# Two-layer streaming encoder, one core: every transfer on SP's queue in program order, stores issued four units late, bias lines made on GpSimd

## The chip, the core and the metric

The kernel runs on one core of a Trainium2 chip. The core has five engines with a queue of instructions each: TensorE (PE in the rows: matmuls, with the weight loads as PEld), VectorE (DVE), ScalarE (ACT), GpSimd (POOL) and SyncE (SP), which here issues the DMA transfers. An engine works through its queue in the order in which the program was built; an instruction that waits for another engine holds up what stands behind it. The metric is the device time of one execution in microseconds, and lower is better.

## The reference, cut to what matters

One inference step of a two-layer encoder, for 256 prompt frames and 32 sample frames together (288 tokens, 1024 features).

```python
# layer 0: 8 heads of chunked attention with a bias by clipped distance (A), 8 heads of stick-breaking (B)
rel  = clip(q_loc[:, None] - k_loc[None, :], -128, 128) + 128
bias = rel_bias[rel]                      # (head, query, key)
s    = q @ k.T * HEAD_DIM ** -0.5 + bias
p    = softmax(where(valid, s, NEG_INF));  out = p @ v
# layer 1: 16 heads of forgetting attention
log_f = log_sigmoid(z + b_f);  cum = cumsum(log_f)
s    = q @ k.T * HEAD_DIM ** -0.5 + cum[q] - cum[k]
# each layer then: 4-head cross-attention into 256 memory tokens, SwiGLU FFN; a final RMSNorm
```

Keys and values of both layers, the log-forget values, and the memory's keys and values are outputs too, beside the activations.

## The kernel before, in words

**Tiling.** Features lie on the 128 partitions and tokens along the free axis, in eight blocks `x[0..7]` of 128x288. A weight matrix is read in **units**: one 128x1024 float32 tile of 512 KB, the eight 128x128 blocks that make one block of 128 output features. `unit` (L132) loads a unit into a buffer `st` (four of them), ScalarE rounds it to `hi` (L141), and VectorE subtracts to get the rest, `lo` (L142). `project` (L151) multiplies it with the activations, which are split the same way: for each of 8 blocks three matmuls, hi times hi, hi times the activations' rest, and lo times hi, so 24 matmuls of 128x288 to a unit.

**What runs between units.** Attention is written as generators. After each unit `project` calls `tick` (L176), which takes one step of every active generator. A step of `attend_prompt` (L359) for a pair of heads: transposes of the values (`vt`) and scores (`sc`), with the softmax on VectorE and ScalarE; one tick later transposes of the weights (`tp`, copied out by ScalarE as `pt`); one tick later the product with the values (`po`). For every second pair, `attend_sample` does the same for the sample frames (`ss`, `ts`, `os`). In `pairs` (L807) eight pairs of heads follow each other: units q, k and v of a pair, then its attention is made active, then units of the memory's keys or values (`Memory.step`, L544).

**What sets the order.** The order in which each engine's instructions stand is not the order of the Python text. The framework schedules the built program by its own costs, engine by engine, and may move an instruction ahead of others where its operands are ready earlier. That holds for SP's transfers also: a load can be put ahead of a store that was written before it.

**The bias of layer 0.** `rel_lines` (L735) makes, for each of 8 heads, a line of 384 values, and writes it 128 times to DRAM, each time shifted by one (`skew`, 385 values to a row), so that a diagonal band can be read as a rectangle. It is called after the first unit of layer 0: SP loads the line (L739), VectorE fills its clipped part (L740), SP stores it (L742) and issues eight copies (L745). `rel_prompt` (L753) reads two rectangles to a head, 128x128 and 128x256, and GpSimd masks two corners.

**The gate of layer 1.** `gate` (L821) takes the forget-gate unit (w[24]) through transposes on PE (`gt`), absolute value, exponential and logarithm on ScalarE and a chain of small VectorE operations to `lf`; SP stores `lf` (L848, L849); after two ticks PE sums it up (`gc`, `gs`, `gn`), VectorE copies the sums out, SP stores them (`cumd`, `cumsd`, L858, L865), and every pair of heads loads its lines from there (`ck`, L896). GpSimd makes the bias tiles (`bc`, L901 to L904).

Of the kernel before, what the change touches and what calls it, by code (L numbers as in the profile page):

```python
# [22 lines left out]
FB = 22  # L23


@with_exitstack
def encoder_step(ctx: ExitStack, tc: tile.TileContext, a):
# [15 lines left out]
    cnt = [0]  # L43

# [31 lines left out]
    def first_part(c0, c1):  # L76
        DMA.dma_start(first[:, c0:c1], a["w_ab"][0][:, c0:c1])

    first_part(0, 256)
    for i in range(4):  # L80
        DMA.dma_start(xh[i], a["xT"][:, 2 * i * NT:2 * (i + 1) * NT])
        if i == 0:
            DMA.dma_start(gain, a["gains"])
            first_part(256, 512)
        if i == 1:
            first_part(512, 1024)
# [5 lines left out]
    make_identity(nc, identb)  # L92

# [23 lines left out]
    for h in range(4):  # L117
        G.memset(odd[32 * h:32 * h + 32, h % 2:h % 2 + 1], 1.0)

# [12 lines left out]
    def unit(src, st=None, pieces=1):  # L132

        if st is None:
            st = wp.tile([P, 1024], F32, tag="st", bufs=4, name=name("st"))
            DMA.dma_start(st, src)
# [48 lines left out]
    def finish():  # L185
        while active:
# [153 lines left out]
    def softmax(s, cols, bias, out):  # L340
# [3 lines left out]
        for i, (c0, c1) in enumerate(cols):  # L344
# [4 lines left out]
            else:  # L349
                V.tensor_tensor_reduce(out=out[:, c0:c1], in0=s[:, c0:c1], in1=bias[:, c0:c1], scale=-1.0, scalar=3e38,  # L350
# [8 lines left out]
    def attend_prompt(q, k, v, vns, j, bias, oh, ol):  # L359

        vn = vns[j] = v_natural(v)
        e = []
        for hd in range(2):
# [5 lines left out]
            softmax(s, QT, bias[hd], e[hd])  # L369
# [134 lines left out]
    def cache(src):  # L504
        t = wk.tile([P, 512], F32, tag="ca", bufs=4, name=name("ca"))
        DMA.dma_start(t, src)
# [12 lines left out]
    class Memory:  # L519
# [5 lines left out]
        def prepare(self):  # L525

            for c in range(2):
                st = wp.tile([P, 1024], F32, tag="st", bufs=4, name=name("mem"))
                DMA.dma_start(st, a["memT"][:, 1024 * c:1024 * c + 1024])
# [14 lines left out]
        def step(self):  # L544
            i, l = self.i, self.l
            self.i += 1
            if i < 8:
# [5 lines left out]
                DMA.dma_start(a["mkT"][l, i], t[:, 0:NP])  # L553
                self.k.append(split(t[:, 0:NP], tok("kh", F32R)[:, 0:NP], tok("kl", F32R)[:, 0:NP]))
            else:
# [13 lines left out]
                if half == 1:  # L569
                    for t in range(2):  # L570
                        v = tok("mv")
                        V.tensor_scalar(v[:, 0:NP], self.p[:, 256 * t:256 * t + 256], memcol[:, t:t + 1], None, op0=ALU.mult)
                        DMA.dma_start(a["mv"][l, t, :, hd * 256:hd * 256 + 256], v[:, 0:NP])
# [151 lines left out]
    def evac_kv(cur, p, dst):  # L725
        t = tok("kv")

        def go():
            V.tensor_tensor(t, p[:, :NT], cur.r, ALU.mult)
            DMA.dma_start(dst, t)  # L730
# [4 lines left out]
    def rel_lines():  # L735


        ln = cst.tile([8, 384], F32, name="line")
        DMA.dma_start(ln[:, 128:384], a["rel"][:, 0:256])  # L739
        V.tensor_copy(ln[:, 0:128], ln[:, 128:129].to_broadcast([8, 128]))  # L740
        d = dr.tile([8, 384], F32, name="lined")
        DMA.dma_start(d, ln)  # L742
        sk = dr.tile([8, 128 * 385], F32, name="skew")
        for h in range(8):
            DMA.dma_start(bass.AP(tensor=sk.tensor, offset=sk.offset + h * 128 * 385, ap=[[385, P], [1, 384]]),  # L745
                          bass.AP(tensor=d.tensor, offset=d.offset + 384 * h, ap=[[0, P], [1, 384]]))
        return sk

    def rel_rows(sk, h, c, rows, n):

# [306 lines left out]
```

## Time and profile before

| what | us |
|---|---|
| median of 3 runs (970.48 to 972.98) | 971.6 |
| the profiled execution, its own time | 974.15 |
| its span, first to last instruction | 972.3 |
| PE busy in the span | 955.3 |
| DVE busy | 588.6 |
| ACT busy | 484.8 |
| POOL busy | 195.1 |

The profile is of one execution. Busy time of PE counts matmuls from start to end, and these overlap, so a share near 100% says that PE had work, not that it ran at its best rate. TensorE's granted clock was 1 in all but the stretches that the prediction shows. Of the span, some 70 us at the front and some 40 us at the start of layer 1 hold nearly all of PE's idle time.

### The profile page before, as it was taken

To read this page: it belongs to the slowest core of one execution; us is meant where nothing else is said; L and a number is where in the kernel's file an instruction comes from. 1 tells how busy PE (TensorE), PEld (TensorE's weight loads), DVE (VectorE), ACT (ScalarE), POOL (GpSimd) and SP (SyncE) were. 2 spreads that over 40 slices of the span, in tenths; PEclk is the share of its full clock that TensorE was granted. 3 is DMA by queue.
4 is the path that set the end of the run, shared out by engine and by line. 5 is a ranking of instruction groups with operands and counts; after the bars stand their busy time and mean duration, and the time that the engine had idled before them with its cause. 6 is when DMAs were issued, how large, how long until landed. Compare 5 with 4: busy or idle time off the path is not lost.

```text
span 972.3 us, 19122 instructions
## 1 busy us (share of the span) xinstructions
PE 955.3 (98%) x7495; PEld 923.2 (95%) x7495; DVE 588.6 (61%) x1133; ACT 484.8 (50%) x856; POOL 195.1 (20%) x291
## 2 busy tenths in 40 slices
PE   8999999999999999999999999999999999999997
PEld 7889999998999999999998999999989999999996
DVE  6587555676666555754565666657757655555452
ACT  5456768545554444444444545446546544444331
POOL 3021001310213222411004333213002222222010
PEclk9999999999999999999999999999999999999999
DMA  7775455544254444554555555555434444444431
GB/s 232 247 241 189 137 180 181 183 162 147 103 174 154 173 162 164 191 192 160 173 202 161 179 190 191 169 164 179 150 117 159 159 159 173 163 164 173 165 117 49
DMA packets 59721, 163.59 MB, mean 168 GB/s; under 512 B 8192, under 2 KB 20528, under 8 KB 59632
## 3 DMA queue, kind: packets, MB, share of 16 engines
q1 hardware_dynamic: 59632, 162.38, 49.0%
q8 instruction: 59, 0.97, 0.4%
q14 instruction: 30, 0.25, 0.1%
HBM read 152.20 MB, written 11.72 MB: 169 GB/s over the span
## 4 chain that ended last, share of the span: by engine, by line
PE 91%; DMA 3%; DVE 3%; issue 1%; ACT 1%; SPq 1%; POOL 0%; DVEq 0%; POOLq 0%; ACTq 0%
PE pj L68 51%; PE dn L68 14%; PE op L68 11%; PE mv L68 5%; PE po L68 1%; PE xo L68 1%; PE xs L68 1%; DMA st<-w_ab 1%; PE zb L68 1%; PE sc L68 1%; DVE lo L142 1%; DMA skew<-lined 1%; DMA x<-xT 1%; PE xss L68 1%; PE xt L614 0%
## 5 line engine op out<-in xcount | busy, mean ns | idle before, releaser
L141 ACT CAST hi<-st 128x1024 fp32r<-128x1024 f32 x260 | 272.2, 1049 | 335.7 <-issue 147.3
L68 PE MATMUL pj<-hh,hi 128*128 128x288 f32 (+1 forms) x1352 | 406.3, 301 | 0.0
L68 PE MATMUL pj<-hl,hi 128*128 128x288 f32 (+1 forms) x1352 | 399.9, 296 | 1.7 <-DVE hl L250 1.7
L68 PE MATMUL pj<-hh,lo 128*128 128x288 f32 (+1 forms) x1352 | 400.2, 296 | 0.0
L142 DVE TENSOR_TENSOR lo<-st,hi 128x1024 fp32r<-128x1024 f32 x260 | 322.7, 1242 | 127.4 <-PE dn L68 41.2
L68 PEld LDWEIGHTS pj<-hh,hi 128*128 128x128 f32 x1352 | 257.0, 190 | 5.8 <-issue 4.2
L68 PEld LDWEIGHTS pj<-hl,hi 128*128 128x128 f32 x1352 | 257.1, 190 | 3.3 <-DVE hl L250 3.2
L68 PEld LDWEIGHTS pj<-hh,lo 128*128 128x128 f32 x1352 | 256.9, 190 | 0.0
L68 PE MATMUL dn<-fh,hi 128*128 128x288 f32 x400 | 108.5, 294 | 0.0
L68 PE MATMUL dn<-fh,lo 128*128 128x288 f32 x352 | 103.3, 294 | 0.0
L68 PE MATMUL dn<-fl,hi 128*128 128x288 f32 x304 | 89.5, 294 | 0.0
L68 PE MATMUL op<-ol,hi 128*128 128x288 f32 x256 | 75.8, 297 | 0.0
L68 PE MATMUL op<-oh,hi 128*128 128x288 f32 x256 | 75.5, 297 | 0.0
L68 PE MATMUL op<-oh,lo 128*128 128x288 f32 x256 | 75.2, 294 | 0.0
L68 PEld LDWEIGHTS dn<-fh,hi 128*128 128x128 f32 x400 | 72.3, 188 | 0.0
L68 PEld LDWEIGHTS dn<-fh,lo 128*128 128x128 f32 x352 | 66.2, 188 | 0.0
L213 POOL TENSOR_TENSOR ssq<-ssq,sq 128x288 f32<-128x288 f32 (+1 forms) x37 | 37.7, 1018 | 119.8 <-ACT sq L202 76.8
L68 PEld LDWEIGHTS dn<-fl,hi 128*128 128x128 f32 x304 | 57.1, 188 | 0.0
L695 POOL TENSOR_TENSOR fl<-us,fh 128x288 fp32r<-128x288 f32 x38 | 32.9, 865 | 119.3 <-ACT fh L694 119.3
L690 DVE TENSOR_TENSOR us<-pj,rstd 128x288 f32<-128x288 f32 x44 | 20.1, 457 | 59.9 <-PE pj L68 59.9
L691 POOL TENSOR_TENSOR gs<-gs,sg 128x288 f32<-128x288 f32 x44 | 38.9, 884 | 75.8 <-ACT sg L689 75.8
L68 PEld LDWEIGHTS op<-ol,hi 128*128 128x128 f32 x256 | 48.2, 188 | 0.6 <-issue 0.4
(257 smaller groups left out, 1204.9 us busy)
## 6 DMA issues: line engine op xcount, KB each, us to landing
st<-w_gate SPq DMA_DIRECT2D x44, 512.0 KB, 3.3
st<-w_up SPq DMA_DIRECT2D x44, 512.0 KB, 3.2
st<-w_down SPq DMA_DIRECT2D x44, 512.0 KB, 3.2
st<-w_c SPq DMA_DIRECT2D x25, 512.0 KB, 3.3
st<-w_ab SPq DMA_DIRECT2D x23, 512.0 KB, 4.4
st<-w_xk SPq DMA_DIRECT2D x16, 512.0 KB, 3.4
st<-w_xv SPq DMA_DIRECT2D x16, 512.0 KB, 3.5
st<-w_xq SPq DMA_DIRECT2D x16, 512.0 KB, 3.5
```

Source lines behind the costliest of these rows:

```text
L68: T.matmul(out, lhsT, rhs, start=start, stop=stop, skip_group_check=True)
L141: S.copy(hi[:, b], st[:, b])
L142: V.tensor_tensor(lo[:, b], st[:, b], hi[:, b].bitcast(F32), ALU.subtract)
L213: eng.tensor_tensor(s[:, :self.n], self.acc[i][:, :self.n], q[:, :self.n], ALU.add)
L690: V.tensor_tensor(us, pu[:, :NT], cur.r, ALU.mult)
L691: G.tensor_tensor(gs, gs, sg, ALU.mult)
L695: G.tensor_tensor(lo, us, hi.bitcast(F32), ALU.subtract)
```

## The change

Four things are done, and the program is scheduled anew.

1. Every transfer that SP issues goes through `move`, which keeps them in the order of the program text (`keep_in_program_order`).
2. The stores of keys, values and memory outputs are put off by four units: `store` puts them on a list of four, and each `tick` issues the oldest entry. `finish` ticks until the list is empty.
3. The bias lines of layer 0 are made at the very front, by GpSimd's own DMA queue and GpSimd's own copy. A head's line is written 64 times and not 128, in two copies of four heads each; a head reads two rectangles of 64x256, and both query tiles take their bias from one 128x256 tile (offsets 128 and 0).
4. Memory preparation is made active just ahead of the third pair's units and not behind the second pair's, the first pair of layer 1 starts one tick later (`later`), the bias tiles of layer 0 are loaded at the attention's first step, and `y` is stored in three transfers and not six.

```diff
+    def move(dst, src):
+        tc.keep_in_program_order(DMA.dma_start(dst, src))
...
+    G.dma_start(line[:, 128:384], a["rel"][:, 0:256])
...
+    G.tensor_copy(line[:, 0:128], line[:, 128:129].to_broadcast([8, 128]))
+    G.dma_start(lined, line)
+    for h in range(0, 8, 4):
+        G.dma_start(bass.AP(tensor=skew.tensor, offset=skew.offset + h * SKEW, ap=[[SKEW, 4], [385, 64], [1, 384]]),
+                    bass.AP(tensor=lined.tensor, offset=lined.offset + 384 * h, ap=[[384, 4], [0, 64], [1, 384]]))
...
             st = wp.tile([P, 1024], F32, tag="st", bufs=4, name=name("st"))
-            DMA.dma_start(st, src)
+            move(st, src)
...
+        for f in stores.pop(0):
+            f()
+        stores.append([])
+    stores = [[] for _ in range(LATE)]
+    def store(dst, t):
+        stores[-1].append(lambda: move(dst, t))
...
     def rel_prompt(h):
+        t = tok("bi")
+        for p in (0, 64):
+            move(t[p:p + 64, 0:256], rel_rows(h, 128 - p, 64, 256))
+        G.memset(t[0:64, 192:256], NEG)
...
-        DMA.dma_start(a["lf"][0:256].rearrange("(t p) h -> p t h", p=P), lf[:, 0:32].rearrange("p (t h) -> p t h", h=H))
-        DMA.dma_start(a["lf"][256:288], lf[0:NS, 32:48])
+        move(a["lf"][0:256].rearrange("(t p) h -> p t h", p=P), lf[:, 0:32].rearrange("p (t h) -> p t h", h=H))
+        move(a["lf"][256:288], lf[0:NS, 32:48])
...
-            return attend_prompt(qs[j], ks[j], vs[j], vns, j, bias, o[0][j], o[1][j])
+            return later(attend_prompt(qs[j], ks[j], vs[j], vns, j, bias, o[0][j], o[1][j]), j == 0)
...
-            DMA.dma_start(a["y"][P * t:min(P * t + P, NT), b], out[r, b])
+        move(a["y"][P * t:min(P * t + P, NT)], out[r])
```

**Place 1: the start of layer 1.** SP's queue before, from the unit of v0 on (`st_6172` is the unit of k0, `st_6231` that of v0, the `w_xk` rows are units of the memory's keys, `w_c` rows are units of layer 1):

```order
L136 DMA st_6172<-w_c 128x1024
L136 DMA st_6231<-w_c 128x1024
L136 DMA st_6265<-w_xk 128x1024
L136 DMA st_6323<-w_xk 128x1024
L136 DMA st_6361<-w_xk 128x1024
```

The store of `lf` stood 12 rows further down. SP's queue of the change at the same place, where `st_6158` is k0, `st_6216` v0 and `st_6401` q1:

```order
L48 DMA st_6158<-w_c 128x1024
L48 DMA lf<-lf 128x2x16
L48 DMA lf<-lf 32x16
L48 DMA st_6216<-w_c 128x1024
L48 DMA st_6249<-w_xk 128x1024
L48 DMA cumd<-gr_6283 16x256
L48 DMA cumsd<-gw_6290 16x160
L48 DMA st_6306<-w_xk 128x1024
L48 DMA st_6343<-w_xk 128x1024
L48 DMA kv<-kv_6214 128x288
L48 DMA ck_6381<-cumd 128x512
L48 DMA st_6401<-w_c 128x1024
```

The loads of v0 and of the first memory unit now stand behind the store of `lf`, the next two memory units behind the store of the sums, and q1 behind the load of the first pair's lines. PE's queue before, around the transposes of the gate (`pj_6237` is v0):

```order
L829 MATMUL gt_6203<-ident,gz_6167 128x16
L830 MATMUL gt_6203<-ident,gz_6167 128x16
L831 MATMUL gt_6203<-ident,gz_6167 32x16
L68 MATMUL pj_6237<-hl_5872,hi_6233 128x288
L68 MATMUL pj_6237<-hh_5871,lo_6234 128x288
```

PE's queue of the change there (`pj_6164` is k0, `pj_6222` v0):

```order
L73 MATMUL pj_6164<-hh_6039,lo_6161 128x288
L847 MATMUL gt_6189<-ident,gz_6153 128x16
L848 MATMUL gt_6189<-ident,gz_6153 128x16
L849 MATMUL gt_6189<-ident,gz_6153 32x16
L73 MATMUL gc_6280<-tri_110,lf 16x256
L73 MATMUL gc_6280<-tri_110,lf 16x128
L73 MATMUL gs_6287<-tri_110,lf 16x160
L73 MATMUL gs_6287<-tri_110,lf 16x32
L73 MATMUL gn_6294<-lf,tri_110 128x16 x3
L73 MATMUL pj_6222<-hh_5395,hi_6218 128x288
```

Before, 50 matmuls of units stood between the last `gt` and the first `gc`; now none does, and v0 comes behind the sums.

**Place 2: the first pair of layer 0.** ScalarE's queue before (`hi_400` is q1's unit, `hi_464` k1's, `hi_510` v1's, `vn` the copy of the transposed values of pair 0):

```order
L141 CAST hi_400<-st_398 128x1024
L202 ACTIVATE sq_232<-x_82 128x288
L141 CAST hi_464<-st_462 128x1024
L280 COPY rstd_380<-nr_376 128x288
L141 CAST hi_510<-st_508 128x1024
L336 COPY vn_433<-vt_429 128x256
L337 COPY vn_433<-vt_429 32x128
```

ScalarE's queue of the change (`hi_454` is k1, `hi_499` v1, `hi_549` q2):

```order
L307 COPY rstd_374<-nr_370 128x288
L363 COPY vn_415<-vt_411 128x256
L364 COPY vn_415<-vt_411 32x128
L158 CAST hi_454<-st_452 128x1024
L158 CAST hi_499<-st_497 128x1024
L158 CAST hi_549<-st_547 128x1024
L380 ACTIVATE e_429,st_430<-e_429,st_430 128x128
```

k1's rounding now stands behind the copy of the values, which itself waits for PE's transposes; PE's k1 unit is the next thing after these and the scores.

**Place 3: pair 1 of layer 0.** PE's queue before, behind the last scores of the sample frames (`ss`; `pj_661` is k2, `tp_694` the transposes of pair 1):

```order
L68 MATMUL ss_638<-ca_559,q_460 32x128
L68 MATMUL ss_638<-kv_505,q_460 32x32
L68 MATMUL pj_661<-hh_166,hi_657 128x288
L68 MATMUL pj_661<-hl_167,hi_657 128x288
L68 MATMUL pj_661<-hh_166,lo_658 128x288
```

PE's queue of the change there:

```order
L73 MATMUL ss_617<-ca_538,q_450 32x128
L73 MATMUL ss_617<-kv_495,q_450 32x32
L403 MATMUL tp_674<-ident,e_596 128x128
L404 MATMUL tp_674<-ident,e_596 128x128
L405 MATMUL tp_674<-ident,e_596 128x128
L403 MATMUL tp_680<-ident,e_608 128x128
L404 MATMUL tp_680<-ident,e_608 128x128
L405 MATMUL tp_680<-ident,e_608 128x128
```

The 24 matmuls of a unit that stood between scores and transposes are gone from there. The same is so for pairs 2 and 3 of layer 0 and for pairs 1, 3, 5 and 7 of layer 1; the number of PE's matmuls is the same in both programs.

More of the change, by code (lines that the diff above doesn't have):

```diff
@@ L23 @@
 FB = 22
+LATE = 4
 @with_exitstack
@@ L92, in encoder_step @@
     make_identity(nc, identb)
+    SKEW = 64 * 385
+    line = cst.tile([8, 384], F32, name="line")
+    lined = dr.tile([8, 384], F32, name="lined")
+    skew = dr.tile([8, SKEW], F32, name="skew")
+    G.dma_start(line[:, 128:384], a["rel"][:, 0:256])
     ntri = cst.tile([P, P], F32, name="ntri")
@@ L338, in v_natural, with softmax @@
         return vn
-    def softmax(s, cols, bias, out):
+    def softmax(s, cols, bias, out, at=None):
         n, rows = len(cols), out.shape[0]
@@ L368, in attend_prompt @@
             e.append(work("e"))
-            softmax(s, QT, bias[hd], e[hd])
+            softmax(s, QT, bias[hd], e[hd], at)
         yield 1
@@ L818, in pairs, with later @@
                 memory.steps(steps[j])
+    def later(g, n):
+        for _ in range(n):
+            yield 1
+        yield from g
     def gate(cur, p, res, lf, bf):
```

74 lines of the change are left out of this document (29 added, 45 removed).

## The prediction

> **What bounds the kernel now.** I read the shares of busy time and the costliest groups first, then the table of stretches for where TensorE is not at its pitch.
>
> ```profile
> PE 955.3 (98%) x7495; PEld 923.2 (95%) x7495; DVE 588.6 (61%) x1133; ACT 484.8 (50%) x856; POOL 195.1 (20%) x291
> L141 ACT CAST hi<-st 128x1024 fp32r<-128x1024 f32 x260 | 272.2, 1049 | 335.7 <-issue 147.3 <-PE pj L68 82.0 <-PE dn L68 43.4
> L142 DVE TENSOR_TENSOR lo<-st,hi 128x1024 fp32r<-128x1024 f32 x260 | 322.7, 1242 | 127.4 <-PE dn L68 41.2 <-issue 35.9 <-PE pj L68 27.0
> core 0: us, PE busy (x) PEld busy (x) DVE busy (x) ACT busy (x) POOL busy (x), PEclk, DMA share, GB/s
> 17.06:34.13 17.07, 15.05 (x118) 14.24 (x116) 9.23 (x30) 5.06 (x14) 1.17 (x8) 1.00 0.86 242
> 34.13:37.50 3.37, 3.35 (x15) 2.96 (x15) 1.42 (x5) 1.91 (x4) 0.00 (x0) 0.50 0.43 143
> 70.00:173.00 103.00, 102.88 (x898) 97.13 (x898) 60.80 (x122) 73.27 (x126) 11.88 (x13) 1.00 0.53 176
> 488.00:525.70 37.70, 34.73 (x268) 32.56 (x267) 23.26 (x61) 19.99 (x34) 5.20 (x11) 1.00 0.57 191
> 525.70:529.10 3.40, 3.40 (x16) 3.40 (x15) 0.68 (x1) 0.19 (x1) 0.00 (x0) 0.51 0.55 146
> 529.10:647.00 117.90, 117.65 (x1034) 108.92 (x1033) 74.27 (x204) 59.56 (x147) 37.47 (x85) 1.00 0.54 184
> ```
>
> TensorE is the bound. From 70 to 173 us it idles 0.12 us of 103, from 529.1 to 647 0.25 of 117.9. It idles 2.0 us between 17.06 and 34.13 and 3.0 us between 488 and 525.7. Directly behind each of these two, the granted clock stands at one half for 3.4 us, which costs about 1.7 us each. DMA, VectorE and ScalarE have slack everywhere else. So the change can win at most what these holes hold; beyond that it can only change how many holes there are. What decides is what stands in PE's queue between an attention's scores and the transposes that wait for its softmax.
>
> **The price of an uncovered softmax.** One pair of layer 0 shows the chain, though a unit stood between:
>
> ```profile
> 27.18 0.27 PE L332 MATMUL vt<-ident,kv 128*128 128x128 f32 x1
> 27.60 0.93 PE L68 MATMUL sc<-kv,q 64*128 64x128 f32 x8
> 30.68 0.36 ACT L336 COPY vn<-vt 128x256 f32<-128x256 f32 x1
> 30.94 0.25 ACT L337 COPY vn<-vt 32x128 f32<-32x128 f32 x1
> 31.95 0.28 DVE L350 CUSTOM_DVE_ANT_0 e<-sc,bi 128x128 f32<-128x128 f32 x1
> 33.92 0.30 PE L374 MATMUL tp<-ident,e 128*128 128x128 f32 x1 [2.02 <-DVE e L355]
> 34.80 0.45 PE L374 MATMUL tp<-ident,e 128*128 128x128 f32 x1
> PE tp L374 <- DVE e L355: 5.0, 6, 2.0
> 524.00 0.30 PE L374 MATMUL tp<-ident,e 128*128 128x128 f32 x1 [1.70 <-DVE e L355]
> L378 ACT COPY pt<-tp 128x384 f32<-128x384 f32 x24 | 10.4, 478 | 1.1 <-PE tp L376 1.1
> L327 ACT CAST oh<-po 128x256 fp32r<-128x256 f32 x16 | 5.9, 370 | 6.2 <-PE po L68 6.2
> L328 DVE TENSOR_TENSOR ol<-po,oh 128x256 fp32r<-128x256 f32 x16 | 6.7, 418 | 2.6 <-ACT oh L327 2.6
> L729 DVE TENSOR_TENSOR kv<-pj,rstd 128x288 f32<-128x288 f32 x32 | 14.3, 449 | 15.1 <-PE pj L68 15.1
> ```
>
> From the first `e` to the first transpose pass 1.97 us (31.95 to 33.92); the second head follows 0.88 us later. Scores of the first head end some 0.5 us before those of the second, and `ss` covers another 0.5 to 0.9. With nothing else between, 1.2 us stay open in the best case, 1.6 where another row lies in VectorE's way.
>
> **Part 1: the front, layer 0.** New idle time of PE, by the changed queues:
> - k1's rounding is now behind `vn`: 0.36 + 0.25 + 1.05 us behind the transposes less 0.93 of scores leaves 0.8 with signals, then `lo` 1.24 less the first matmuls 0.9: 1.7.
> - End of pair 0: the products wait for `pt` (0.48), and v1's copy `kv` (0.45) stands behind `ol` (0.42) and `oh` (0.37), with PE's `po` beside them: 1.6.
> - Pair 1: softmax 1.6, second head 0.5, the sample's `ts` 0.25; then k2's `hi` and `lo`, which stand behind the copies of `pt` and behind a row that waits for `os`, 1.2: 3.6.
> - Pair 2: 1.6 for the softmax, 0.15 at the sums, 0.9 for `pt`, 0.6 for the next unit's `lo`: 3.3.
> - Pair 3: 1.2 + 0.5 + 0.25, and 1.0 for the next `lo`: 3.0.
>
> That is 13.2 us. Three of these holes are as long as the one ahead of 34.13, and I charge 1.7 us of half clock for each: 5.1. What goes: PE's waits for VectorE at the transposes, six with 5.0 us in all, less 1.7 and a small one at 524 in layer 1, so 3.2 at the front, and the old half clock of 1.7: together 4.9. **Front: +13.4.**
>
> The bias moves to GpSimd's own queue. The trace of before has no transfer of GpSimd's; the nearest are SP's:
>
> ```profile
> 13.74 5.05 SPq L745 DMA_DIRECT2D skew<-lined  x8
> skew<-lined SPq DMA_DIRECT2D x8, 192.0 KB, 6.9
> cumd<-gr SPq DMA_DIRECT2D x1, 16.0 KB, 1.8
> ```
>
> Half the bytes are written. Bound below: a copy lands like the 16 KB one in 1.8 us; above: it takes 6.9 as now and the issue another 5.05, so the lines lie ready at 20 at the earliest and 27 at the latest if the eight-row line is made near 13. I take about 21, since two issues stand for eight. Program order puts k1's load behind the first bias loads, so late bias holds up k1: k1's `hi` waits for `vn` until about 28.2 anyway, and less some 4.5 us of issue and landing (3.3 below) that leaves cover until some 23.6. At 27 k1 would come 3.4 us late, which the range keeps. (The Trainium skill, "DMA: Bandwidth & Descriptors", section on the software path of GpSimd, puts a fixed cost near 2 us on such a transfer and a slower first byte than a hardware queue's; three in a row would by that end some 2 us after my 21, inside the cover. No trace of before shows it.)
>
> **Part 2: the start of layer 1.** The gate's chain, which was hidden by 50 matmuls, now stands in the open, with v0's load behind its end.
>
> ```profile
> 501.38 0.17 PE L831 MATMUL gt<-ident,gz 16*32 16x16 f32 x1
> 503.60 1.04 ACT L141 CAST hi<-st 128x1024 fp32r<-128x1024 f32 x1
> 506.84 1.16 DVE L142 TENSOR_TENSOR lo<-st,hi 128x1024 fp32r<-128x1024 f32 x1
> 508.63 0.21 DVE L847 SCALAR_TENSOR_TENSOR lf<-gate_z,gate_l 128x48 f32<-128x48 f32 x1
> 508.87 0.40 SPq L848 DMA_DIRECT2D lf<-lf  x1
> 508.89 0.82 PE L68 MATMUL gc<-tri,lf 128*16 128x256 f32 x4 [1.12 <-DVE lf L847]
> 509.32 0.46 SPq L849 DMA_DIRECT2D lf<-lf  x1
> 28.70 0.29 PE L68 MATMUL pj<-hl,hi 128*128 128x288 f32 x1
> 28.83 0.29 PE L68 MATMUL pj<-hh,lo 128*128 128x288 f32 x1
> 530.00 0.88 PE L68 MATMUL po<-pt,vn 128*64 128x256 f32 x8
> st<-w_c SPq DMA_DIRECT2D x25, 512.0 KB, 3.3
> ```
>
> From the last `gt` to `lf` pass 7.3 us (501.55 to 508.84); without the `hi` and `lo` between (which wait for loads that are now behind) and with their handovers 5.45 remain. In the changed queue the transposes end near 499.9 (16 matmuls fewer stand ahead of them, 2.1 us, less 0.5 for their handover), so `lf` is ready near 505.3 and the two stores of 0.40 and 0.46 are issued by 506.2. v0's load lands 3.3 later, `hi` 1.05, `lo` 1.24: v0 starts at 510.75, and its third matmul at 511.95. From there to the products of pair 0 (`po`) the changed queue holds 168 matmuls of units at 0.13 us, 22.0, and 3.4 us of transposes, scores and products: 536.2 had nothing waited. Idle are the 0.9 behind v0's first `lo`, 2.7 at the memory unit whose load stands behind the stored sums (1.8 for its `hi`, 0.9 for its `lo`), and a half clock of 2.3 (two holes near each other): 542.1, where before ended them at 530.9. **+11.1**, rounded down. If the loads lagged by one more landing this would be 14.4; if v0's load were issued on time, the chain of 5.45 less the sums' own 1.6 would cost about 4.
>
> **Part 3: pairs of layer 1.** Pair 1 has tp behind `ss` with nothing between, and po behind that: 1.6 + 0.5 + 0.25 + 0.5 + 0.9 as above, 3.75. Pairs 3, 5 and 7 hold one exposure each: `kv` ahead of `vt` 0.55, softmax 1.2, second head 0.45, the next `lo` 0.55, so 2.7 each. Together 11.9, and two spells of half clock 3.4. **+15.3.** The even pairs keep 24 matmuls (3.2 us) between scores and transposes, and cost nothing.
>
> **Part 4: the rest.** In cross-attention of both layers a unit's load now waits for a buffer that `xso` frees (two such waits of loads in before, 11.8 us, on SP alone): 0.4 us each, +0.8. The stores, four units late, are issues of 0.3 to 0.6 us on SP, which waits anyway:
>
> ```profile
> SPq L136 <- DVE lo L142: 583.8, 218, 10.1
> SPq L506 <- PE xso L68: 11.8, 2, 5.9
> 966.70 3.07 SPq L976 DMA_DIRECT2D y<-yo  x6
> ```
>
> Waiting of 584 us shows that loads start when a buffer frees, not when SP has time; the four units (13 us) of delay let a store find its data ready. Lower bound 0, upper bound one unit's 3.2 us for each of eight pairs. I take 0, the nearer row being the waiting. At the end three stores stand for six: issues of 0.5 us, one and a half of them saved on the last path, −0.7.
>
> **Sum.** 13.4 + 11.1 + 15.3 + 0.8 − 0.7 = +39.9. The profiled execution took 974.15 and lies 2.55 over the median of 971.6, so I set the sum against the profile, 1014.0, and give it on the median's footing: **1011.5**, 4.1% slower.
>
> **Rivals.**
> - *The holes cost no half clock.* In before, 2.02 us of idle were followed by the half clock, so I charge it. Without it 5.1 + 3.4 + 2.3 fall away: 1001. Against it speak the stretches at 34.13 and 525.70, for it that holes of 0.67 us left the clock at 1. The Trainium skill's page "TensorE: Matmul & The Clock Gate", section "Why this matters for your kernels", has the clock drop only for gaps over about 3 us; by that rule the new holes, each under it, would be free. The row at 34.13 disagrees with it.
> - *Half the holes are covered.* VectorE and ScalarE run in the gaps undisturbed, and a chain may take 1.4 us and not 1.97, and `lo` may come sooner. Half of parts 1 and 3, 14.3, goes: about 997.
> - *Program order starves the loads.* A store whose tile is late holds up every load behind it; one unit's 3.2 us at four odd pairs gives 1024, at six with k1 3.4 late 1034. For it: the sums' stores and the `ck` loads stand ahead of loads. Against: the 584 us of waiting.
> - *Faster.* The two old holes close, since bias is ready before it is wanted: 2.0 + 1.2 + 1.7 at the front, 3.0 + 1.7 at 488, and 0.7 at the end, about −9, so 962. That holds only if the rows of PE that now wait find their softmax ready because the weights are late anyway; it decides as soon as new waits sum to under 9 us. Pair 1's and the gate's chains alone come to that, so I give it little.
> - *The change does not do what it says.* If bias by GpSimd came at 27 or later, k1 comes 3.4 later and nothing of the softmax is ready sooner: 1015, inside the forecast's own range.
>
> **Chances.** Forecast 1003 to 1020: 0.48. No half clock, or half the holes: 0.32 (988 to 1003). Starved loads: 0.13 (1020 to 1034). Faster 0.05, no change 0.02. A measurement of this kernel tells some 0.3% from no change. Range: 985 to 1028 holds all of the first two and the lower end of the third, and leaves out some 0.17. Slower 0.93, same 0.02, faster 0.05.
>
> **What would show it.** PE's waits at the transposes on VectorE (5.0 us in all in before) should grow to 12 or more, spread over seven pairs. The half-clock stretches should be more than two, each behind a hole of 2 us. v0 of layer 1 should start 9 to 12 us after the last `gt`, with v0's load issued behind the store of `lf`. The first bias row should come before 26 us. The feed-forward stretches should keep their lengths. If PE's new waits name loads at the even pairs also, the stores starve the loads; if PE's idle time stays under 6 us in all, the order of queues was no guide to what waits, and the forecast is wrong from its first step.

## The result, and the profile after

The change made the kernel slower by 6.9%: 1038.7 us (median of 4 runs, 1037.2 to 1039.8) against 971.0 us, ratio 1.069, 95% interval 1.067 to 1.072. The prediction was 1011.5 us with a range up to 1028: the right sign, but 27 us short. The profiled execution has a span of 1038.1 us against 972.3, so 65.8 us are to be found.

The shares of busy time and the two costly groups of the changed kernel, as quoted for before (unit splitting is now on lines 158 and 159, PE's helper on line 73):

```profile
PE 980.5 (94%) x7495; PEld 936.6 (90%) x7495; DVE 597.1 (58%) x1132; ACT 483.3 (47%) x856; POOL 195.5 (19%) x288
L159 DVE TENSOR_TENSOR lo<-st,hi 128x1024 fp32r<-128x1024 f32 x260 | 325.9, 1256 | 116.8 <-ACT hi L158 50.2
L158 ACT CAST hi<-st 128x1024 fp32r<-128x1024 f32 x260 | 270.6, 1048 | 242.0 <-issue 82.8
```

The work is the same, 7495 matmuls, yet PE is busy 25 us longer and idle some 41 us longer. A stretch in which PE idles is called a hole below. The table of stretches, cut at the same matmuls in both kernels, says where. The columns are the stretch, its length, the busy time of PE, PEld, DVE, ACT and POOL, the granted clock, the DMA share and GB/s. Before:

```profile
20.00:86.04 66.04, 62.85 (x517) 56.69 (x517) 44.74 (x135) 33.20 (x83) 8.85 (x22) 0.97 0.76 242
86.04:173.44 87.40, 87.28 (x750) 82.78 (x750) 49.48 (x85) 64.68 (x105) 11.14 (x12) 1.00 0.50 163
493.58:530.88 37.30, 34.33 (x255) 31.70 (x253) 22.26 (x58) 19.21 (x32) 6.61 (x14) 0.95 0.53 171
530.88:646.72 115.84, 115.59 (x1015) 107.32 (x1016) 73.36 (x203) 58.68 (x146) 36.07 (x83) 1.00 0.53 182
646.72:756.33 109.61, 109.56 (x852) 105.49 (x851) 74.51 (x143) 57.66 (x113) 17.24 (x16) 1.00 0.43 148
```

The changed kernel:

```profile
20.00:99.04 79.04, 68.81 (x521) 59.25 (x520) 47.37 (x136) 32.82 (x82) 7.83 (x14) 0.94 0.48 156
99.04:192.48 93.44, 89.03 (x751) 83.52 (x751) 47.96 (x85) 64.53 (x104) 11.21 (x12) 1.00 0.46 155
515.05:564.27 49.22, 37.82 (x255) 34.21 (x254) 20.72 (x56) 16.36 (x29) 10.59 (x24) 0.86 0.46 145
564.27:705.71 141.44, 128.04 (x1016) 114.63 (x1016) 77.74 (x204) 61.64 (x148) 32.03 (x72) 0.93 0.44 147
705.71:821.28 115.57, 112.28 (x852) 107.31 (x851) 76.29 (x144) 58.91 (x115) 16.15 (x16) 0.99 0.47 166
```

The differences of the lengths, beside what the prediction had (its part and term):

| stretch | predicted, us | measured, us |
|---|---|---|
| front, pairs 0 to 3 of layer 0 | +13.4 | +13.0 |
| stick-breaking pairs 4 to 7 of layer 0 | 0 | +6.0 |
| cross-attention of layer 0, up to layer 1 | +0.4 | +2.4 |
| start of layer 1, up to pair 0's products | +11.1 | +11.9 |
| the other pairs of layer 1 | +15.3 | +25.6 |
| cross-attention of layer 1 | +0.4 | +6.0 |
| feed-forward of layer 1, tail | −0.7 | +0.9 |

Of PE's idle time some 7 us lie in the last stretch of each kernel, at the very end (7.1 of the 17.0 us before, 7.3 in the changed kernel), so they are no part of the loss.

PE's longest waits, first rows of the view (engine and instruction, what it waited for, sum, times, longest):

```profile
PE tp L403 <- DVE e L383: 12.5, 11, 2.2
PE gc L73 <- DVE lf L865: 5.6, 1, 5.6
PE pj L73 <- ACT hi L158: 4.9, 3, 2.4
PE pj L73 <- DVE lo L159: 3.9, 6, 1.1
```

These are the waits that the prediction named: transposes waiting for their softmax (5.0 us before, 12.5 now), the sums of the gate waiting for `lf`, units waiting for their split. One pair of layer 1, in order of time:

```profile
606.54 0.93 PE L73 MATMUL sc<-kv,q 64*128 64x128 f32 x8
607.61 0.29 DVE L378 CUSTOM_DVE_ANT_0 e<-sc,bc 128x128 f32<-128x128 f32 x1 [1.60 <-PE sc L73]
609.16 0.55 DVE L383 TENSOR_SCALAR e<-e,st 128x128 f32<-128x128 f32 x2
609.59 0.30 PE L403 MATMUL tp<-ident,e 128*128 128x128 f32 x1 [1.69 <-DVE e L383]
```

The chain from the first `e` to the first transpose takes 1.98 us, as the 1.97 of the prediction, and 1.69 of it stay open.

### The profile page after: what moved, and what is told of

Its sections match the earlier page's. It is cut to its first block, busy times and chain, and to the rows that moved or that the text cites. A ratio compares the mean times of both kernels' runs of the same rounds, so it can differ in the third digit from the quotient of the medians.

```text
span 1038.1 us, 19058 instructions
## 1 busy us (share of the span) xinstructions
PE 980.5 (94%) x7495; PEld 936.6 (90%) x7495; DVE 597.1 (58%) x1132; ACT 483.3 (47%) x856; POOL 195.5 (19%) x288
## 4 chain that ended last, share of the span: by engine, by line
PE 76%; ACT 6%; DMA 6%; DVE 5%; issue 1%; SPq 1%; DVEq 0%; ACTq 0%
PE pj L73 44%; PE dn L73 13%; PE op L73 8%; PE mv L73 3%; ACT hi L158 2%; DVE lo L159 2%; DMA st<-w_ab 2%; PE po L73 1%; DMA st<-w_xk 1%; DMA st<-w_oab 1%; DMA st<-w_xv 1%; ACT e L380 1%; PE sc L73 1%; DMA st<-w_xo 1%; PE xs L73 1%
## 5 line engine op out<-in xcount | busy, mean ns | idle before, releaser
L73 PEld LDWEIGHTS pj<-hh,hi 128*128 128x128 f32 x1352 | 259.0, 192 | 10.2 <-ACT hi L158 6.0
L240 POOL TENSOR_TENSOR ssq<-ssq,sq 128x288 f32<-128x288 f32 (+1 forms) x37 | 37.5, 1014 | 120.8 <-ACT sq L229 88.1
L344 POOL TENSOR_TENSOR kl<-mk,kh 128x256 fp32r<-128x256 f32 x16 | 14.1, 884 | 201.5 <-ACT kh L343 190.6
```

Of the source, the lines that this page charges most:

```text
L73: T.matmul(out, lhsT, rhs, start=start, stop=stop, skip_group_check=True)
L240: eng.tensor_tensor(s[:, :self.n], self.acc[i][:, :self.n], q[:, :self.n], ALU.add)
L344: eng.tensor_tensor(lo, t, hi.bitcast(F32), ALU.subtract)
```

## The experiments

Each ran beside the kernel before on the same chip; that took 973.0 to 973.9 us there, median of each job. Lags below are those of the profiled runs: how much later than in the kernel before the same matmul starts.

**Which part costs?** Four kernels take the kept order or the bias lines away, or do one alone.

`e1_free`, the change without the kept order:

```
     def move(dst, src):
-        tc.keep_in_program_order(DMA.dma_start(dst, src))
+        DMA.dma_start(dst, src)
```

> The change with its transfers not kept in the order of the text; late stores, bias lines by GpSimd and the moved places stay. Theory (the kept order alone opens the holes in PE's queue, by putting transposes directly behind scores): the queue has its units between again, PE's idle time falls under 12 us, the front's old stall of 2.0 us and its half clock are gone too: 962 to 972 us. Rival (late stores, GpSimd's bias or the moved places cost by themselves): 985 us or more, with waits left in PE's queue.

Measured 993.3 us, ratio 1.020 (1.018 to 1.023). All that the change had cost behind the front is gone: from pair 4 of layer 0 (lag 19.0) to the end (19.8) nothing is lost. But the front itself lags 19 us, more than in the change, so the rival is half right: something else costs too. DMAs issued between 12 and 27 us, with their time from issue to landing:

```profile
st<-w_ab SPq DMA_DIRECT2D x3, 512.0 KB, 10.6
skew<-lined POOLq DMA_DIRECT2D x2, 384.0 KB, 10.2
ca<-cab SPq DMA_DIRECT2D x2, 256.0 KB, 10.1
```

The same stretch of the kernel before:

```profile
st<-w_ab SPq DMA_DIRECT2D x3, 512.0 KB, 4.3
skew<-lined SPq DMA_DIRECT2D x8, 192.0 KB, 6.9
```

A weight unit takes 10.6 us to land here while GpSimd's copies are under way. Three units, two cache loads and a memory tile are in flight with them, and of the three units of the kernel before two were issued ahead of SP's copies (the third took 6.5 us), so the copies' own share is not shown. VectorE, whose queue has the norm's chain behind this unit's `lo`, lets PE's `nr` wait 5.3 us. The first bias tile is loaded at 49 us, behind the weights, and the transposes of pair 0 wait 4.4 us.

`e5_bias_alone`, the kernel before with the bias part only (as in the diff of the change, with plain `dma_start`):

> The kernel before with only the bias part of the change: lines by GpSimd's own queue at the front, 64 rows, two 64x256 loads to a head; no kept order, no late stores. Theory (GpSimd's two copies run beside the first weights, take their bandwidth, and the planner, free to order, puts the bias loads behind five weights): the front costs 15 to 20 us as in the run without kept order, the rest is as before: 985 to 994 us. Rival (the bias part is harmless or gains the old stall, and the 20 us of that run come from late stores and moved places): 964 to 974 us.

Measured 988.9 us, ratio 1.017 (1.014 to 1.019): 20.3 us of lag at pair 4, of which some 2 are given back later. The bias part alone costs 15.4 us, most of the 20.3 that `e1_free` lost, by the same holes:

```profile
28.51 1.49 PE L68 MATMUL nr<-ident,y 128*128 128x128 f32 x6 [4.08 <-DVE y L244]
48.75 0.58 PE L68 MATMUL pj<-hh,hi 128*128 128x288 f32 x1 [2.26 <-DVE q L735]
61.15 0.45 PE L387 MATMUL tp<-ident,e 128*128 128x128 f32 x1 [4.29 <-DVE e L368]
```

`e6_free_oldbias`, `e1_free` with the old bias lines; what is left is late stores, moved places and three stores of `y`:

```
-    G.dma_start(lined, line)
...
+            if j == 0:
+                proj.line = rel_lines()
```

> The change without kept order and with the bias lines of the kernel before: late stores, moved places, three stores of y stay. Theory (these cost nothing by themselves): 968 to 974 us, the front within 2 us of before. Rival (late stores or the moved places make the 20 us): 985 us or more.

Measured 971.6 us, ratio 0.998 (0.997 to 0.999). These parts cost nothing.

`e7_rows64`, the kernel before with 64 rows and two 64x256 loads to a head, still on SP and in the old place:

```
-            DMA.dma_start(bass.AP(tensor=sk.tensor, offset=sk.offset + h * 128 * 385, ap=[[385, P], [1, 384]]),
+            DMA.dma_start(bass.AP(tensor=skew.tensor, offset=skew.offset + h * SKEW, ap=[[385, 64], [1, 384]]),
```

> The kernel before with 64 rows to a line and two 64x256 loads to a head, but still on SP's queue and in the old place. Theory (what hurts is GpSimd's early copies and the planner's belief in them, not the smaller form): half the bytes land sooner, the stall of 2.0 us at the first transposes and its half clock of 1.7 go in part: 967 to 972 us. Rival (smaller descriptors and more issues make the bias later, or the planner moves the transposes): 976 us or more.

Measured 972.0 us, ratio 0.999 (0.998 to 1.000): no loss, and a gain that cannot be told from none. So two parts cost, and they are not independent: the bias lines on GpSimd's queue with a free order (15 to 20 us, all at the front), and the kept order. How much of the first comes from weights that land late, and how much from bias loads put behind them, no run separates.

**Are the loads late, or is the queue wrong?** `e2_pe_text` keeps SP's order and puts PE's instructions in the order of the text too:

```
-        T.matmul(out, lhsT, rhs, start=start, stop=stop, skip_group_check=True)
+        tc.keep_in_program_order(T.matmul(out, lhsT, rhs, start=start, stop=stop, skip_group_check=True))
...
-            T.transpose(t[:, 0:128], e[hd][:, 0:128], ident)
+            tc.keep_in_program_order(T.transpose(t[:, 0:128], e[hd][:, 0:128], ident))
```

> The whole change, SP's order kept, and PE's matmuls and transposes kept in the order of the text as well, so that a unit stands between scores and transposes again. Theory (the weights are in time on the chip, and only the hoisted transposes wait): the holes of all pairs vanish, those at the start of layer 1 stay or grow, since v0 waits for its load behind the store of the log-forget values: 985 to 1000 us. Rival (the loads themselves are late in the kept order): the holes move from the transposes to the units, PE's waits name hi or lo, 1020 us or more.

Measured 1053.8 us, ratio 1.083 (1.081 to 1.085). By the number the rival won, but the trace gives it only one of its places. From pair 2 of layer 1 to the end of the pairs the loss falls from 18.1 to 7.3 us: there the hoisted transposes were the loss. At the start of layer 1 the loads are late indeed: v0 waits 11.0 us for its `hi`, issued behind the store of `lf`. In layer 0 (19.3 us from pair 1 to pair 4, against 13.0) neither theory fits. In order of time, SP's load of k2 and what stands around its `hi`:

```profile
32.56 0.93 SPq L48 DMA_DIRECT2D st<-w_ab  x2
51.56 0.41 ACT L380 ACTIVATE es<-es,st 128x160 f32<-128x160 f32 x1
51.98 0.40 ACT L229 ACTIVATE sq<-mem 128x256 f32<-128x256 f32 x1
52.28 1.03 ACT L158 CAST hi<-st 128x1024 fp32r<-128x1024 f32 x1
53.36 0.61 PE L73 MATMUL pj<-hh,hi 128*128 128x288 f32 x1 [3.59 <-ACT hi L158]
```

k2 was issued at 32.6, and loads of that time landed in 6.5 us. Its `hi` ran at 52.3 without a wait of its own: it stood behind the exponentials of pair 1 in ScalarE's queue. The scheduler had placed the split on ScalarE and VectorE behind the softmax as well, as if the load came late; on the chip it had come 13 us earlier. Putting PE's queue alone back exposes the split in place of the softmax. A part of the loss is the text order's own: PE waits 7.0 us for `xe` in the two cross-attentions, a wait that neither the kernel before nor the change has. The text order without the kept order of SP was not run.

`e3_small_free` leaves bias, cache and line loads (`bi`, `bs`, `ca`, `ck`, `bcs`, `cq`) out of the kept order:

```
-            move(ck, bass.AP(tensor=cp.tensor, offset=cp.offset + 512 * j, ap=[[0, P], [1, 512]]))
+            DMA.dma_start(ck, bass.AP(tensor=cp.tensor, offset=cp.offset + 512 * j, ap=[[0, P], [1, 512]]))
```

> The change, but bias, cache and line loads (bi, bs, ca, ck, bcs, cq) are not kept in order; weights and stores are. Theory (in layer 1 the odd pairs' holes come from the weights being put behind the ten small loads of the sample frames): the 25 us of layer 1's pairs go, the front and the start of layer 1 stay as in the change: 1010 to 1018 us. Rival (stores among the weights make the order): 1030 us or more.

Measured 1018.2 us, ratio 1.047 (1.045 to 1.050). PE's queue has the units back between scores and transposes in layer 1, and from pair 2 to the end of the pairs 1.4 us are lost and not 18.1. Front and start of layer 1 stay. The time is at the upper edge of what was expected.

**What does a hole cost beside itself?** `e4_fill` puts 24 matmuls without use into unused columns ahead of the transposes:

```
             t = att("tp")
+            if hd == 0 and (j % 2 == 1 or (at and j > 1)):
+                for _ in range(24):
+                    mm(t[:, 384:512], identb, identb)
```

> The change, with 24 small matmuls without use put ahead of the first transposes of pairs 2 and 3 and the odd pairs, into unused columns of the same PSUM tile: the softmax is as late, but PE does not idle. Theory (a hole of about 1.7 to 2.2 us costs itself and then 1.7 us of half clock): the transposes come at the same time, and 7 to 9 half-clock stretches go, 12 to 16 us: 1022 to 1027 us. Rival (the half clock has another cause than PE's idleness, or 1.3 us of filling is not enough): 1036 us or more.

Measured 1032.6 us (1029.6 to 1040.7), ratio 1.062 (1.058 to 1.067): less than was expected: 6 us and not 12 to 16. The traced run took 1040.7 us, no less than that of the change (1039.8), so the trace shows the clock behind each hole and not where the median gained. The six us at pair 5 of layer 1, in the change and then with the filling:

```profile
645.90:651.90 6.00, 4.12 (x19) 3.43 (x20) 5.45 (x17) 6.00 (x15) 0.00 (x0) 0.72 0.32 90
```

```profile
653.00:659.00 6.00, 4.94 (x46) 4.08 (x44) 5.45 (x17) 6.00 (x16) 0.00 (x0) 1.00 0.36 79
```

The softmax comes no sooner, VectorE and ScalarE do the same, but the clock stays at 1 (0.72 in the change). Where a hole was filled the half clock was gone at six stretches of 1.7 us, 10 us in all; where a second hole follows (`ts` of layer 1's pair 1) it stayed, and 7 us of it came at places that the filling does not touch (front, layer 0's cross-attention, start of layer 1). With the 1.7 us that are gone at layer 1's `mv`, this trace has 5 us of half clock less and no time gained; what took them back is not shown. That the hole causes the half clock is shown; that each hole costs 1.7 us is not, it comes and goes, by a rule that the last section works out.

**The places one by one.** `e9_lf_late` puts the store of `lf` off like the other stores:

```
-        move(a["lf"][256:288], lf[0:NS, 32:48])
+        store(a["lf"][256:288], lf[0:NS, 32:48])
```

> The change with one more store put off: the log-forget values wait four units like the other stores, so that the loads of v0 and the first memory unit no longer stand behind them; the stored sums stay where they were. Theory (the 5.6 us hole behind the gate's transposes and the 1.8 us before v0 come from v0's load standing behind that store): both go, and one or two half-clock stretches: 7 to 11 us, 1027 to 1032 us. Rival (the hole only moves to the memory units behind the stored sums, which wait longer): 1035 us or more.

Measured 1032.7 us (1029.6 to 1036.6), ratio 1.061 (1.059 to 1.064), just above the theory's range. The holes of 5.6 and 1.8 us are gone, one of 4.2 stands at a memory unit behind the stored sums. Up to the end of the pairs, layer 1 loses 28.9 us and not 37.5. Both theories have a part: the store made some 9 of that place's 12 us.

`e10_oldbias_kept` keeps the order, with the old bias lines in it:

```
+        for h in range(8):
+            move(bass.AP(tensor=sk.tensor, offset=sk.offset + h * 128 * 385, ap=[[385, P], [1, 384]]),
```

> The change with the bias lines of the kernel before, made on SP behind the first unit, all in the kept order. Theory (in layer 0 the first weights stand behind bias loads that wait for GpSimd's copies, and this is what puts transposes directly behind scores and brings later weights late): the 13 us up to the end of pair 3 become 5 or less, the rest stays: 1025 to 1031 us. Rival (the kept order alone costs layer 0 that much, and SP, held by the eight copies and their readiness, delays k0 and v0): 1037 us or more.

Measured 1037.2 us, ratio 1.066 (1.065 to 1.068): the rival's number. But layer 0 differs: from pair 1 to pair 4 nothing is lost (lag 9.4 to 8.9; the change 0.0 to 13.0), and the 9 us come ahead of it, where k0 waits for a load that stands behind the eight copies:

```profile
13.53 5.04 SPq L48 DMA_DIRECT2D skew<-lined  x8
18.78 1.27 SPq L48 DMA_DIRECT2D st<-w_ab  x2
28.70 0.61 PE L73 MATMUL pj<-hh,hi 128*128 128x288 f32 x1 [8.12 <-ACT hi L146]
```

The two units issued behind these copies took 8.8 and 9.2 us to land, so weights behind such copies are late on SP's queue too.

In the kept order, then, the bias part opens the holes of pairs 1 to 3, and without it the old lines cost nearly as much in another place.

`e13_xv_free` leaves only the loads of `w_xv` out of the kept order:

```
-                w = unit(a["w_xv"][l, hd, half])
+                w = unit(a["w_xv"][l, hd, half], keep=False)
```

> The change with the loads of w_xv alone not kept in order, so that the two of each cross-attention come ahead of the cache loads that wait for a buffer. Theory (the prediction's step on cross-attention was right in place and too small in size: the units land late, 2.4 us of holes each and a half clock): the steps of both cross-attentions, 2.4 and 6 us in the change, fall under 1.5 each: 5 to 8 us less, 1030 to 1034 us. Rival (the holes there come from the memory units' place on ScalarE): 1037 us or more.

Measured 1030.0 us, ratio 1.057 (1.056 to 1.059). Layer 1's cross-attention now loses nothing (109.5 us long, 109.6 before; 6.0 lost in the change), and the stretch ahead of it, from pair 6 on, where the first of these units is, 1.7 (6.3); layer 0's loses 1.5, all of it in the output projection ahead (2.4). In the change these loads stood behind cache loads that wait for a buffer, as SP's queue and PE's first `mv` show:

```profile
762.40 0.81 SPq L48 DMA_DIRECT2D ca<-cmv  x2
763.31 0.84 SPq L48 DMA_DIRECT2D st<-w_xv  x2
769.09 1.04 ACT L158 CAST hi<-st 128x1024 fp32r<-128x1024 f32 x1 [1.42 <-DMA st<-w_xv]
770.19 0.39 PE L73 MATMUL mv<-hi,hh 128*128 128x256 f32 x1 [1.49 <-ACT hi L158]
```

`e12_three_undone` undoes three at once in the kept order (old bias lines, small loads free, `lf` late):

```
-    G.dma_start(lined, line)
...
+        move(d, ln)
...
-            move(ck, bass.AP(tensor=cp.tensor, offset=cp.offset + 512 * j, ap=[[0, P], [1, 512]]))
+            DMA.dma_start(ck, bass.AP(tensor=cp.tensor, offset=cp.offset + 512 * j, ap=[[0, P], [1, 512]]))
...
-        move(a["lf"][256:288], lf[0:NS, 32:48])
+        store(a["lf"][256:288], lf[0:NS, 32:48])
```

> The kept order with late stores, three things undone: bias lines as in the kernel before, small loads free, log-forget store put off. Theory (the places add up: the gains of the three runs taken alone, near 10, 20 and 8 us, sum): 998 to 1006 us, with the stick-breaking pairs, the cross-attention and the stored sums left over. Rival (the places share one cause, and undoing one gives most of it): either under 985 or over 1012 us.

Measured 1006.3 us (1002.4 to 1009.9), ratio 1.034 (1.031 to 1.037), 32 us under the change. The gains alone were 1.5, 20.6 and 6.1, in sum 28; the time is at the upper edge of the theory's range. Within what the runs scatter the places add up.

**The stores.** `e8_stores_now` issues each store at once, `e14_stores_free` keeps the delay but leaves stores out of the kept order:

```
-        stores[-1].append(lambda: move(dst, t))
+        move(dst, t)
```

```
-        stores[-1].append(lambda: move(dst, t))
+        stores[-1].append(lambda: DMA.dma_start(dst, t))
```

> The change with the stores of keys, values and memory outputs issued at once, in the kept order. Theory (a store whose tile is not ready holds every load behind it, and four units of delay soften that): loads later in every pair, more holes before units: 1055 us or more. Rival (the late stores are themselves a cost, by standing among later loads): 1030 us or less.

> The change with its late stores (four units) not kept in order; all loads stay in order. Theory (with four units of delay a store finds its data ready, and the prediction's 0 for the stores was right): 1033 to 1041 us, the stick-breaking pairs' 6 us stay. Rival (late stores still hold loads in layer 0, where the copies they wait for are late themselves): 1028 us or less, with the stick-breaking pairs' 6 us gone.

`e8_stores_now` took 1455.0 us, ratio 1.493 (1.488 to 1.499): in a kept order, stores at once would have cost 416 us more, and the delay of four units is what makes the order bearable. PE waits for `hi` 163 us there:

```profile
PE pj L73 <- ACT hi L158: 163.3, 38, 6.3
ACT hi L158 <- DMA st<-w_c: 93.3, 18, 13.0
```

`e14_stores_free` took 1046.9 us, ratio 1.075 (1.074 to 1.077), slower than the change: k1 waits 6.5 us at the front, and the first sample of layer 1 waits 2.7 us for a cache load. The stick-breaking pairs lose 3.5 us, with 6.0 in the change: neither what the theory expected nor what the rival did. SP still waits 56.5 us there before stores of keys, values and memory keys, so the freed stores did not stop holding up loads, and the run settles little.

**A better version.** `e11_best`: late stores, moved places, three stores of `y`, lines of 64 rows on SP in the old place, no kept order.

```
-        tc.keep_in_program_order(DMA.dma_start(dst, src))
+        DMA.dma_start(dst, src)
...
-    G.dma_start(lined, line)
...
+        for h in range(8):
+            DMA.dma_start(bass.AP(tensor=skew.tensor, offset=skew.offset + h * SKEW, ap=[[385, 64], [1, 384]]),
```

> Late stores, moved places and three stores of y without kept order, with lines of 64 rows made on SP in the old place. Theory (the parts that cost nothing add their small gains): 968 to 971 us, under the kernel before by 0.2 to 0.5%. Rival (both gains are the same one, or the planner puts the two halves of a bias tile further back): 972 to 976 us.

Measured 970.9 us, ratio 0.998 (0.997 to 0.999) over 12 runs: faster than the kernel before by 0.2%. PE's waits at the prompt's transposes fall from 5.0 to 1.8 us, those at the sample's rise from 0.2 to 1.8, and the half clock behind pair 0 is gone. The gain is no larger than that of `e6_free_oldbias`.

```profile
PE tp L395 <- DVE e L375: 1.8, 4, 0.9
```

## Why the prediction was right or wrong

**The bound and the mechanism: right.** The time of PE's queue is the time of the kernel, and the change opened holes in it by moving transposes, the gate's sums and units to where they wait. `e1_free` and `e6_free_oldbias` show that kept order and bias lines together are the whole loss.

**Part 1, front (+13.4, measured +13.0): right in size, in part by luck.** The holes are where the list had them: 0.7 and 0.7 for k1's split (1.7 predicted), 0.2 and 1.3 at the end of pair 0 (1.6), 1.9, 2.2 and 1.9 at the transposes of pairs 1, 2 and 3, and 1.1 at k2's `lo`. They sum to 10 against 13.2, and three steps of 1.7 us of half clock are the 5.1 charged, though not one to a hole: one behind pair 1, two behind pair 2, none behind pair 3. The last 3 us lie in wider spaced matmuls that no row of its own shows. That the sum agrees is luck: the holes were 3 us too large in the list, and these 3 us were not in it. But the softmax that lies open was not the cause to be undone: `e2_pe_text` covered it and lost more, since the split was queued behind it too. The bias lines were ready when supposed: the two copies landed at 18.8 and 20.8 us, against 21 taken, and SP, which had stood before them for 12.8 us, issued the first bias load at 18.84. What the prediction did not see is that the same lines cost 15 to 20 us in a free order, where weights and cache loads are issued beside the copies; in the kept order no weight is issued until they have landed.

**Part 2, start of layer 1 (+11.1, measured +11.9): right by two errors that cancel.** v0's load was issued at 527.66, behind the store of `lf` at 526.66, and v0 started at 532.15, 11.0 us after the last `gt` had ended (9 to 12 foretold). The chain from `gt` to the sums took 5.6 us of waiting (5.45 taken). The half clock there was 6.8 us where 2.3 was charged; the holes were the shorter for it. `e9_lf_late` shows the store as the cause.

**Part 3, pairs of layer 1 (+15.3, measured +25.6): the failed step.** The holes came out as worked in sum: those over 0.2 us make 12.7 against 11.9. But the hole at each softmax was longer, 1.69 to 1.84 us in pairs 3, 5 and 7 where 1.2 stood, with none for the second head. The sentence that failed is "two spells of half clock 3.4": the stretch has 10.2 us of half clock, six times 1.7, at these places of the changed kernel:

```profile
569.91:576.74 6.83, 6.01 (x24) 4.84 (x25) 4.35 (x7) 4.01 (x6) 0.00 (x0) 0.50 0.23 78
610.87:614.28 3.41, 2.95 (x14) 2.66 (x13) 2.91 (x5) 3.41 (x7) 0.00 (x0) 0.50 0.37 119
648.42:651.83 3.41, 2.92 (x14) 2.63 (x13) 3.18 (x5) 3.41 (x7) 0.00 (x0) 0.50 0.38 118
685.97:692.79 6.82, 5.96 (x28) 5.91 (x28) 4.19 (x7) 3.68 (x7) 0.00 (x0) 0.50 0.22 77
```

Every odd pair had at least one step of 3.4 us, pairs 1 and 7 two. In the kernel before one hole of 2.02 and one of 1.70 had been followed by it; I charged it to the longest holes only, though 1.7 us was on the list. Over the whole kernel it makes 23.8 us where 10.8 were charged, so half of the 26 us that the sum was short. `e4_fill` shows it to follow from the holes. The other 2 to 3 us of the stretch no row of its own shows.

**Part 4: the other half.** Cross-attention was right in place and mis-sized: 0.8 us for two, measured 8.4. A late unit costs its `hi` and its `lo` (1.5 and 0.9 in layer 1) and 1.7 of half clock; `e13_xv_free` takes layer 1's part away, and of layer 0's 2.4 about one. For the stick-breaking pairs, 6.0 us, the prediction had no term and gave no reason for leaving them out; its nearest term, the stores, it took at 0. Over 99 to 192 us the changed kernel shows, on ScalarE and on SP:

```profile
ACT hi L158 <- DMA st<-w_xk: 7.3, 2, 4.4
SPq L48 <- DVE mk L581: 31.8, 5, 9.5
SPq L48 <- DVE kv L758: 29.3, 6, 8.7
```

Before had no wait of `hi` for a load in that stretch. With the kept order SP stands 61 us before stores whose data is not ready (25 us before, where it stood 40 us more before loads, for a buffer to come free), units come late, and what stands behind their `hi` on ScalarE (`sw`, for which PE's `po` waits 1.45 us) comes late with them. The prediction had named such a cost of the stores, with 3.2 us for each of eight pairs as its upper bound, and not taken it. `e14_stores_free` did not isolate it, so its share remains argued, and which transfer costs these 6 us stays open. The tail, −0.7, was +0.9 with the feed-forward.

**The rivals.** "The holes cost no half clock" fell: by the rule of the Trainium skill ("TensorE: Matmul & The Clock Gate", section "Why this matters for your kernels") holes under about 3 us leave the clock alone, and the trace disagrees: in the changed kernel eight spells of half clock stand behind holes between 1.49 and 2.42 us. "Half the holes are covered" fell as well. "Program order starves the loads" was right about the start of layer 1 and the cross-attentions, where PE waits for units whose loads stood behind others; at the odd pairs, where it put its price, PE waits for the softmax. Its number, 1024 to 1034, was nearer than the forecast's. The items of "Faster" add up to 10.3 us and not 9, which changes no forecast. Why the scheduler reckoned loads late that were in time on the chip is not shown by any run.

## What to carry to other kernels

Before pinning the order of one queue, look at what the scheduler then does with the others: here it moved transposes on PE and splits on ScalarE as if the transfers landed late, and the loss shows where nothing was pinned. In a queue kept in program order one entry that waits holds up all behind it: delay stores until their data is surely there, and put loads that wait for a buffer behind those that do not. When TensorE gets holes, charge each hole and the clock that it costs: here every hole about as long as one that had cost half clock before, and two short ones close together as one.

## What the runs showed of the hardware

The half clock follows holes far shorter than expected, but not always. Every hole of PE of 2.4 us or more was followed by clock 0.5 for 3.4 us or a multiple of that, and each 3.4 us cost up to 1.7. Between 1.5 and 2.3 us it depends on where the hole falls. In each of the sixteen traces all changes of the granted clock lie whole multiples of 3.413 us apart, and what goes with half clock is PE's idle time within one step of that length, not the length of a hole. Three steps of the changed kernel (columns as above):

```profile
81.81:85.22 3.41, 2.49 (x34) 1.83 (x32) 2.44 (x12) 1.74 (x8) 0.00 (x0) 1.00 0.20 70
85.22:88.63 3.41, 2.46 (x15) 1.60 (x17) 3.15 (x12) 3.41 (x11) 0.00 (x0) 1.00 0.35 132
607.46:610.87 3.41, 1.54 (x24) 1.03 (x23) 2.88 (x17) 2.93 (x10) 0.00 (x0) 1.00 0.29 77
```

The hole of 1.87 us at pair 3 of layer 0 is cut by the end of a step into 0.92 and 0.95, and no half clock follows. The hole of 1.69 us at pair 3 of layer 1 lies whole in one step, with 0.18 more, and the next step runs at 0.50. Counted over the sixteen traces from 15 us on, none of 4279 steps at full clock with under 1.09 us of idle was followed by half clock, 12 of 66 with 1.09 to 1.64 us were, and 114 of 115 with more. Once the clock is at one half, 0.7 us of idle in a step kept it there for the next, 113 times of 113. These idle times rest on modelled ends of matmuls, and the counts are of these kernels only.

So the same hole costs one time and not another: 2.17 us at pair 2 of layer 0 was followed by half clock in the change (1.92 us of idle in one step) and by none in `e3_small_free` (1.33 and 1.07); 2.26 us behind `q` by half clock in `e5_bias_alone` (2.14) and by none in `e1_free` (1.51 and 0.74); 1.49 us at `mv`, with 0.87 close behind it, by half clock in the change (2.21) and by none in `e3_small_free` (1.00 and 1.36). Where the steps fall differs from trace to trace, which can make kernels with such holes scatter: the part of layer 0's cross-attention, with the same instructions, lost 2.4 us in the change and 8.0 in `e9_lf_late`, where 3.4 us of half clock were added.

Weight units of 512 KB that are issued while DRAM-to-DRAM copies in pieces of 1.5 KB are under way land late: 10.6 us with two copies of 384 KB on GpSimd's queue (`e1_free`, where cache loads are in flight too), 8.8 and 9.2 us behind eight copies of 192 KB on SP's queue (`e10_oldbias_kept`). Two units issued just ahead of SP's copies took 3.2 and 4.3 us in the kernel before. So the lateness is not GpSimd's alone.
